# Down projection of a gated MLP: from one output pair at a time to one key at a time, with products summed in PSUM

## Chip, cores and metric

The kernel runs on one NeuronCore of a Trainium2 chip. The metric is the device time of one execution in microseconds (us). Before the change it took 1750.57 us (median of 3 runs, 1750.38 to 1752.44).

## The reference

One decoder layer over 1024 tokens (and 16 meta tokens) of width 1024: a projection, three parallel branches, a merge, an output projection, and then the MLP, which the change concerns.

```python
def rms_norm(x, g):
    xf = x.astype(jnp.float32)
    y = xf * lax.rsqrt(jnp.mean(xf * xf, axis=-1, keepdims=True) + EPS)
    return (y * g.astype(jnp.float32)).astype(x.dtype)
...
    hn = rms_norm(h, norm2_g)
    gate, up = jnp.split(hn @ w_gate_up, 2, axis=-1)
    return h + (jax.nn.silu(gate) * up) @ w_down
...
    return rms_norm(h, final_g)[:, N_META:]
```

`w_down` is 2816 x 1024. The result of `@ w_down` is added to the residual `h`, and the sum is normalised over the 1024 features of each token.

## The kernel before

Everything is kept transposed: features on partitions, tokens along the free dimension, in two halves of 512 tokens (`ch` 0 and 1). Every float32 factor is split in a high half, rounded to the matmul's format (ScalarE, a cast), and a low half, the rest (VectorE, a subtraction, L295, in `factor` and `sub_lo`); a product of two split factors takes three matmuls (L268, L269, L270 in `gemm`).

The MLP multiplies 2 x 2 blocks by seven products in place of eight. A block product is one call of `gemm`: four 128-deep steps (three in the last group) of three matmuls each. Its weight factor is one of seven sums of the four weight blocks of an output pair (features `o` and `o + 4`, in units of 128), and its other factor is one of seven **keys**: `B11`, `B21`, `T1`, `B22`, `T2`, `T3`, `T4`, sums of the four activation blocks. The products are numbered 0 to 6 like the keys in `keys`.

The loop over `f` (L2153 on) computes gate and up, 21 steps of seven products, and writes the key tiles (one per key and per pair `p` of feature blocks, 128 x 512) to DRAM: products of activations in `put`, their four sums in `act_sums` on GpSimd, the stores through `stores` on the SP queue. The down projection follows in the same loop. Its 11 pairs `p` form three **groups** (`GR`: 4, 4 and 3 pairs). For a group, all its key tiles (28, or 21) are resident; for each of four output pairs, the seven products run over the group, and `consume_down` adds them to the four result tiles of the pair in SBUF, some through VectorE from PSUM (L1825), some through GpSimd from a temporary (L2010). The weight sums of a pair are made on GpSimd in `pair_sums` (L1909 to L1912), three to four products ahead (`AHEAD`).

When the last output pair of a group starts, `next_group` queues the loads of all the next group's keys into the same buffers, key by key as each is used for the last time, and `split_x` splits a tile at each step of a product (L2090 on ScalarE, L295 on VectorE, every fourth tile on GpSimd). Tiles of `T2`, `T3` and `T4` have their low halves in buffers named `y`; `whi`, `wlo`, `op` are buffers of weight factors; `sw` are weight sums, `raw` loaded weights, `h` and `y` results, `c` temporaries.

In the last group five products per pair run over all 1024 tokens' results as usual. The other two (keys `B21` and `T4`) come at the very end for all four pairs, for tokens 0 to 255 and then 256 to 511 of the first half, with 256-column matmuls. Around them stands the final norm: squares on ScalarE, column sums on TensorE against a column of ones (L1642), the root (L593 to L598), a transposed broadcast on TensorE (L1661), scaling (L2124, L2126) and stores, for the three parts (`ALL1` and two of 256 tokens) one after another.

The program gives the order on each engine by the order in which it is written (`manual_schedule`); every engine and every DMA queue works in order.

## Time and profile before

| | us |
|---|---|
| median of 3 runs | 1750.57 |
| profiled execution, its own time | 1750.45 |
| its span, first to last instruction | 1748.7 |
| TensorE busy | 1667.2 (95%) |
| VectorE busy | 1344.6 (77%) |
| GpSimd busy | 881.0 (50%) |
| ScalarE busy | 763.0 (44%) |
| mean granted TensorE clock | 0.984 |

Durations come from the profiled execution, whose time is within 0.2 us of the median. In rows of single instructions the columns are start, duration, engine, line, operation, output <- inputs, count, and in brackets the idle time before it with what ended it. In rows of groups they are the same names, then busy time and mean in ns, then idle time. In rows of stretches: the window, its length, busy time and number of instructions of PE (TensorE), PEld (weight loads), DVE (VectorE), ACT (ScalarE) and POOL (GpSimd), the granted clock, the share of the DMA engines and GB/s. TensorE's matmuls are pipelined, so their durations overlap, and the distance of two starts is the pace.

### The profile page before, as it was taken

Reading aid. Unit: us, or ns where it says so; the run is one execution under the profiler, and the core shown is the slowest. Engines: PE = TensorE matmul, PEld = TensorE weight load, DVE = VectorE, ACT = ScalarE, POOL = GpSimd, SP = SyncE. Lnnn points to the kernel's source line nnn. Section 1 sums busy time; section 2 is a strip of 40 time slices with the busy share of each in tenths; the row PEclk is TensorE's granted clock in tenths of the full one; section 3 lists DMA queues with packets and bytes.
Section 4 is the critical chain, followed back from the end, with each engine's and each line's share of the span. In section 5 each row is a group of like instructions: output and inputs, shape, how many; then the busy total and the mean of one; then the engine's idle time right before and its main releaser. Section 6 shows DMA issues by size and latency. Waiting matters only on the chain.

```text
span 1748.7 us, 22588 instructions
## 1 busy us (share of the span) xinstructions
PE 1667.2 (95%) x7912; PEld 1383.0 (79%) x7912; DVE 1344.6 (77%) x2100; ACT 763.0 (44%) x1439; POOL 881.0 (50%) x639
## 2 busy tenths in 40 slices
PE   6989999998999999999999998999999999898986
PEld 5778878886888887888778876788888888686866
DVE  7999996588888744888886248777777777979697
ACT  4566217456544444876622234323322324443343
POOL 4322325315555665211174136766666665697664
PEclk9989999999999999999999998999999999999998
DMA  4111123233323333310285431332333226453423
GB/s 148 49 37 33 40 85 108 69 127 101 115 97 112 118 109 119 89 53 1 85 286 184 160 102 38 109 115 91 102 103 126 93 95 233 152 199 121 145 97 115
DMA packets 91922, 190.65 MB, mean 109 GB/s; under 512 B 9552, under 2 KB 21840, under 8 KB 91808
## 3 DMA queue, kind: packets, MB, share of 16 engines
q1 hardware_dynamic: 88704, 184.13, 31.7%
q10 hardware_dynamic: 2992, 4.75, 0.7%
q8 instruction: 62, 1.02, 0.2%
q0 software_dynamic: 112, 0.33, 0.1%
q14 instruction: 52, 0.43, 0.1%
HBM read 135.43 MB, written 53.74 MB: 108 GB/s over the span
## 4 chain that ended last, share of the span: by engine, by line
PE 62%; DVE 7%; DMA 2%; issue 2%; ACT 1%; POOL 1%; DVEq 0%; ACTq 0%; SPq 0%; POOLq 0%
PE ps L268 18%; PE ps L270 18%; PE ps L269 18%; PE ps L1446 2%; DMA y<-T 1%; DVE y L295 1%; PE ps L1422 1%; PE ps L1423 1%; PE ps L1421 1%; PE ps L1470 1%; PE ps L1471 1%; PE ps L1472 1%; DVE y L1712 1%; DVE h L1825 1%; DMA s<-y 1%
## 5 line engine op out<-in xcount | busy, mean ns | idle before, releaser
L268 PE MATMUL ps<-xh,whi 128*128 128x512 f32 (+1 forms) x492 | 175.0, 356 | 4.7 <-DVE u L863 2.4
L270 PE MATMUL ps<-xh,wlo 128*128 128x512 f32 (+1 forms) x492 | 173.9, 354 | 1.1 <-DVE wlo L239 1.1
L269 PE MATMUL ps<-xl,whi 128*128 128x512 f32 (+1 forms) x492 | 174.0, 354 | 0.6 <-POOL xl L295 0.4
L1825 DVE TENSOR_TENSOR c<-c,ps 128x512 f32<-128x512 f32 x175 | 119.4, 682 | 54.3 <-PE ps L270 49.6
L1847 POOL TENSOR_TENSOR h<-c,c 128x512 f32<-128x512 f32 x44 | 68.9, 1585 | 120.8 <-issue 75.1
L1834 ACT ACTIVATE c<-c 128x512 f32<-128x512 f32 x44 | 27.8, 632 | 207.5 <-DVE c L1825 207.5
L268 PEld LDWEIGHTS ps<-xh,whi 128*128 128x128 f32 x492 | 93.6, 190 | 17.8 <-DVE u L863 2.7
L270 PEld LDWEIGHTS ps<-xh,wlo 128*128 128x128 f32 x492 | 93.7, 190 | 14.9 <-DVE wlo L239 1.9
L269 PEld LDWEIGHTS ps<-xl,whi 128*128 128x128 f32 x492 | 93.7, 191 | 13.3 <-POOL xl L295 1.3
L239 POOL TENSOR_TENSOR wlo<-raw,whi 128x1024 fp32r<-128x1024 f32 x21 | 51.7, 2461 | 98.9 <-ACT whi L233 98.9
L269 PE MATMUL ps<-l,whi 128*128 128x512 f32 x232 | 90.9, 392 | 1.3 <-DVE l L295 1.2
L268 PE MATMUL ps<-h,whi 128*128 128x512 f32 x232 | 91.0, 392 | 0.0
L270 PE MATMUL ps<-h,wlo 128*128 128x512 f32 x232 | 90.6, 391 | 0.0
L720 DVE TENSOR_SCALAR_CACHE_REDUCE B<-sc,s 128x912 bf16<-128x912 f32 (+2 forms) x93 | 89.0, 957 | 0.1
L295 DVE TENSOR_TENSOR wlo<-sw,wlo 128x512 fp32r<-128x512 f32 (+1 forms) x49 | 57.1, 1165 | 22.7 <-ACT wlo L1782 19.5
L295 DVE TENSOR_TENSOR op<-raw,op 128x512 fp32r<-128x512 f32 (+1 forms) x42 | 56.3, 1352 | 17.0 <-ACT op L1047 17.0
L295 DVE TENSOR_TENSOR whi<-sw,whi 128x512 fp32r<-128x512 f32 (+1 forms) x50 | 50.6, 1013 | 24.4 <-ACT whi L1782 21.5
L295 DVE TENSOR_TENSOR op<-sw,op 128x512 fp32r<-128x512 f32 (+1 forms) x48 | 52.0, 1088 | 20.1 <-ACT op L1782 19.5
L295 DVE TENSOR_TENSOR whi<-raw,whi 128x512 fp32r<-128x512 f32 (+1 forms) x40 | 53.2, 1331 | 14.2 <-ACT whi L1047 12.7
L2010 POOL TENSOR_TENSOR h<-h,c 128x512 f32<-128x512 f32 x27 | 43.8, 1636 | 31.3 <-DVE c L1825 23.7
L1132 ACT COPY c<-ps 128x512 f32<-128x512 f32 x52 | 30.4, 585 | 63.8 <-PE ps L270 63.7
L1453 POOL CAST pm<-pm 16x512 fp32r<-16x512 f32 x14 | 8.5, 604 | 97.2 <-ACT pm L1449 97.2
(615 smaller groups left out, 5710.8 us busy)
## 6 DMA issues: line engine op xcount, KB each, us to landing
raw<-in_wts_dram SPq DMA_DIRECT2D x136, 512.0 KB, 3.9
T<-h SPq DMA_DIRECT2D x44, 256.0 KB, 5.3
B<-h SPq DMA_DIRECT2D x33, 256.0 KB, 2.0
y<-T SPq DMA_DIRECT2D x33, 256.0 KB, 5.7
y<-b SPq DMA_DIRECT2D x32, 256.0 KB, 2.2
s<-y SPq DMA_DIRECT2D x32, 256.0 KB, 4.9
ga<-c SPq DMA_DIRECT2D x16, 256.0 KB, 3.9
gb<-c SPq DMA_DIRECT2D x16, 256.0 KB, 4.1
```

What stands on the lines that cost most here:

```text
L239: e.tensor_tensor(l[:, c], r[:, c], h[:, c].bitcast(F32), op=ALU.subtract)
L268: nc.tensor.matmul(ps[:, :n], wh, xh, start=(start and k == 0), stop=False, **kw)
L269: nc.tensor.matmul(ps[:, :n], wh, xl, start=False, stop=False, **kw)
L270: nc.tensor.matmul(ps[:, :n], wl, xh, start=False, stop=(stop and k == last), **kw)
L295: getattr(self.nc, eng).tensor_tensor(lo, x, hi.bitcast(F32), op=ALU.subtract)
L720: nc.vector.tensor_scalar(junk2[:, :nk_of(i)], self.sc[i], value, None, op0=ALU.is_ge, op1=ALU.add, accum_out=at(cs, i))
L1132: nc.scalar.copy(t, ps)
L1446: nc.tensor.transpose(p3[:rows, h, :], d["S"][h][:, col:col + rows], self.ident)
L1825: nc.vector.tensor_tensor(dst, a, b, op=ALU.add)
L1834: nc.scalar.activation(t, t, AF.Silu)
L1847: nc.gpsimd.tensor_tensor(t, u, s, op=ALU.mult)
L2010: nc.gpsimd.tensor_tensor(a, a, b, op=ALU.add)
```

## The change

The down projection gets a loop of its own. Its order is now group, key, output pair: a key of a group serves all four pairs in four successive products (**slots**), and then its tiles are done with. Three sets of key buffers rotate (`B11`, `B21`, `T1`), and a table of events (`when`, `run_events`) issues loads at given slots: key tiles one per slot, two keys ahead, and their split three slots after the load at the earliest, at two places of a product. Weight blocks are loaded singly, and their sums are made in place on GpSimd (`down_sums`, `down_factor`), four per pair and group as before.

Each pair has three PSUM chains per group. Products 0, 4, 5 and 6 are added up in one bank, 2 and 3 in another, and 1 has its own. After every product `evict` adds the bank as it then stands to the one result tile that needs this partial sum (`TILE`), on VectorE; the adds of `consume_down` on GpSimd are gone. A product may write a bank only after the eviction of the product before it in that bank.

The keys run in the order `DOWN` (0, 4, 5, 6, 1, 2, 3). Of the last group, the first token half is finished after product 1 and is normalised and stored during the last keys (`out0`). The last key (product 3, which completes features 0 to 511 of the second token half) runs in two token parts of 256, each with four products; the first part's column sums stand in the second part. The outputs read the broadcast scale straight from PSUM; only one pair of outputs at the end goes through ScalarE and GpSimd.

The core of the diff:

```diff
-ORDERS = ((0, 1, 2, 3, 4, 5, 6), (0, 1, 6, 2, 3, 4, 5), (0, 2, 3, 4, 5))
-ALL1 = (1, 0, 512)
-PARTS = (ALL1, (0, 0, 256), (0, 256, 256))
+ORDERS = ((0, 1, 2, 3, 4, 5, 6), (0, 1, 6, 2, 3, 4, 5))
+DOWN = (0, 4, 5, 6, 1, 2, 3)
...
-            nc.tensor.matmul(ps[:, :n], wh, xh, start=(start and k == 0), stop=False, **kw)
...
+            nc.tensor.matmul(ps[:, c0:c0 + n], wh, xh, start=(start and k == 0), stop=False, **kw)
...
-        plans = [(j, 512) for j in range(1, NFF)] + [(NFF + 4 * g + o, P * len(GR[g])) for g in range(len(GR)) for o in range(4)]
+        plans = [(j, 512) for j in range(1, NFF)]
...
+        def weight_tile(kind, o):
+            return self.t(self.xb, [P, 512], tag={"12": "T2h", "21": "T4h", "22": "B22h", "s2": "B22l"}[kind] + str(o))
+
+        def load_w(g, kind, o):
+            n = len(GR[g]) * P
+            off = self.at["wd", (g, o + 4 * (kind[0] == "2"))]
+            src = self.a["wts"][off:off + 2 * n * P].rearrange("(p n) -> p n", p=P)
+            if kind == "11":
+                if o % 2 == 0:
+                    pair = self.t(self.wp, [P, 1024], tag="raw", bufs=2)
+                    W[g, "11", o], W[g, "11", o + 1] = pair[:, :n], pair[:, 512:512 + n]
+                t = W[g, "11", o]
...
+                t = W[g, kind, o] = weight_tile(kind, o)[:, :n]
+            c = n * (kind[1] == "2")
+            nc.sync.dma_start(t, src[:, c:c + n])
+
+        def load_x(q, k):
+            g, kk = divmod(q, NK)
+            key = ("B11", "B21", "T1")[q % 3]
+            pool = self.xb if key == "T1" else self.xap
+            hi, lo = (self.t(pool, [P, 512], F32R, tag=f"{key}{x}{k}") for x in "hl")
+            nc.sync.dma_start(lo.bitcast(F32), xd[keys[DOWN[kk]], GR[g][k]])
+            XQ.setdefault(q, []).append((hi, lo))
+            splits.append((slot, hi, lo))
+
+        def split_x(k):
+            if splits and splits[0][0] + 3 <= slot:
+                _, hi, lo = splits.popleft()
                 x = lo.bitcast(F32)
                 nc.scalar.copy(hi, x)
-                self.sub_lo(lo, x, hi, eng=eng)
+                self.sub_lo(lo, x, hi)
...
+        def down_sums(g, o):
+            pool_op(W[g, "11", o], W[g, "11", o], W[g, "21", o], ALU.subtract)
+            t = W[g, "s2", o] = weight_tile("s2", o)[:, :len(GR[g]) * P]
+            pool_op(t, W[g, "22", o], W[g, "11", o], ALU.subtract)
+
+        def down_factor(g, i, o):
+            made.append(self.factor(W[g, {0: "11", 4: "s2", 5: "11", 6: "22", 1: "12", 2: "21", 3: "s2"}[i], o]))
+            if i == 0 and o >= 2:
+                down_sums(g, o - 2)
+            elif i == 4 and o < 2:
+                down_sums(g, o + 2)
+            elif i == 5:
+                pool_op(W[g, "21", o], W[g, "21", o], W[g, "22", o], ALU.add)
+            elif i == 1:
+                pool_op(W[g, "s2", o], W[g, "12", o], W[g, "s2", o], ALU.subtract)
...
+        for g in range(NG):
+            for i in DOWN:
+                for o in range(4):
+                    thunks.append(lambda g=g, i=i, o=o: down_factor(g, i, o))
+        for o in range(4):
+            when(-14 + o, load_h2, "11", o)
+            when(-11 + o, load_h2, "12", o)
+            when(-7 + o // 2, load_w, 0, "11", o)
+            when(-4 + o // 2, load_w, 0, "21", o)
+            when(-2 + o // 2, load_w, 0, "22", o)
+            when(1 + o, load_h2, "22", o)
+            when(4 + o, load_h2, "21", o)
+            when(8 + o, load_w, 0, "12", o)
+            for g in range(1, NG):
+                t = SLOTS * (g - 1) + o
+                when(t + 11, load_w, g, "11", o)
+                when(t + 15, load_w, g, "22", o)
+                when(t + 18, load_w, g, "21", o)
+                when(t + 22, load_w, g, "12", o)
+        for q in range(NG * NK):
+            for k in range(len(GR[q // NK])):
+                when(-6 + k // 2 if q == 0 else -3 + k if q == 1 else 4 * (q - 2) + k, load_x, q, k)
...
+        TILE = {0: (0, 0), 1: (0, 0), 4: (0, 1), 3: (0, 1), 5: (4, 1), 2: (4, 1), 6: (4, 0)}
+
+        def evict(g, i, o, ps):
+            squares()
+            d, ch = TILE[i]
+            t = h2[o + d, ch]
+            nc.vector.tensor_tensor(t, ps, t, op=ALU.add)
+            if g == NG - 1 and i in (6, 1, 2):
+                sqs.append((o + d, ch))
+
...
+        def stat(accs):
+            return self.row_rstd(accs, self.const)
...
+        def bcast(st, n):
+            ps = self.ps()
+            for j in range(n // P):
+                nc.tensor.transpose(ps[:, j * P:(j + 1) * P], st[:, 8 + j:9 + j].to_broadcast([P, P]), self.ident)
+            return ps
...
+        def out0(o):
+            x = h2[o, 0]
+            nc.vector.scalar_tensor_tensor(x, x, self.cols["fg"][:, o:o + 1], rbs[0], op0=ALU.mult, op1=ALU.mult)
+            nc.sync.dma_start(self.a["out"][o * P:(o + 1) * P, :512], x)
...
+                self.later.append(lambda f=f, i=i: consume(f, i))
+
+        banks = {}
+        for slot in range(NG * SLOTS - 4):
+            g, r = divmod(slot, SLOTS)
+            kk, o = divmod(r, 4)
+            i, q = DOWN[kk], NK * g + kk
+            n_done += 1
+            ahead(n_done - 1 + AHEAD)
+            run_events()
...
+            at = {k: lambda k=k: split_x(k) for k in (0, 2)}
+            if g == NG - 1 and r == 22:
+                at[0] = lambda: sts.update({0: stat([held[0, 1], held[0, 0]])})
+            if g == NG - 1 and r == 23:
+                at[1] = lambda: rbs.update({0: bcast(sts[0], 512)})
+                at[2] = lambda: [out0(x) for x in range(2)]
+            chain = (g, o, 0 if i in (0, 4, 5, 6) else i if i == 1 else 2)
+            old = banks.get(chain)
+            ps = banks[chain] = self.gemm(made.popleft(), XQ[q], 512, at, ps=old, start=old is None, add=old is not None)
+            self.later.append(lambda g=g, i=i, o=o, ps=ps: evict(g, i, o, ps))
...
+        def finish(part, o, ps):
+            c = slice(256 * part, 256 * part + 256)
+            squares()
+            t = h2[o, 1][:, c]
+            nc.vector.tensor_tensor(t, ps[:, c], t, op=ALU.add)
+            sq = sq1[part, o] = ct()[:, :256]
+            nc.scalar.activation(sq, t, AF.Square)
+
+        def stat1(part):
+            sts[1, part] = stat([held[1, 1][:, 256 * part:256 * part + 256]] + [sq1[part, o] for o in range(4)])
+
...
+        todo = {(0, 0): {0: lambda: [out0(x) for x in (2, 3)]}, (0, 1): {0: lambda: out0(4)},
+                (0, 2): {0: lambda: out0(5), 1: prescale}, (0, 3): {0: lambda: out0(6)}, (1, 0): {1: lambda: out0(7)},
+                (1, 1): {1: lambda: stat1(0)},
+                (1, 3): {0: lambda: rbs.update({(1, 0): bcast(sts[1, 0], 256)})}}
+        for part in range(2):
+            c = slice(256 * part, 256 * part + 256)
             for o in range(4):
-                for j, kk in enumerate(("B21", "T4")):
-                    ps = self.gemm(two[o][j], xs[kk], n, at.get((key, o, j)))
-                    self.later.append(lambda o=o + 4 * j, ps=ps, key=key: finish(o, ps, key))
-                for x in after.get((key, o), ()):
-                    out(*x)
+                xs = [(h[:, c], l[:, c]) for h, l in XQ[q]]
+                ps = banks[g, o, 2]
+                self.gemm(fac[o], xs, 256, todo.get((part, o)), ps=ps, start=False, add=True, c0=256 * part)
+                self.later.append(lambda part=part, o=o, ps=ps: finish(part, o, ps))
```

On VectorE, at the first change from the old to the new group, stood these rows before (low halves of key tiles `B22l`, `y` with `T2h` and `T3h`, of factors `wlo`, `whi`, and an addition to a result `y04`):

```order
L295 TENSOR_TENSOR B22l2_2686_13345<-B22l2_2686_13345,B22h2_2685_13344 128x512
L295 TENSOR_TENSOR wlo_2715_13438<-sw_2666_13270,wlo_2715_13438 128x512
L295 TENSOR_TENSOR y14_2695_13383<-y14_2695_13383,T2h0_2694_13382 128x512
L295 TENSOR_TENSOR y15_2697_13386<-y15_2697_13386,T2h1_2696_13385 128x512
L295 TENSOR_TENSOR y16_2699_13389<-y16_2699_13389,T2h2_2698_13388 128x512
L295 TENSOR_TENSOR whi_2718_13466<-sw_2665_13269,whi_2718_13466 128x512
L295 TENSOR_TENSOR y00_2708_13427<-y00_2708_13427,T3h0_2707_13426 128x512
L295 TENSOR_TENSOR y01_2710_13430<-y01_2710_13430,T3h1_2709_13429 128x512
L1825 TENSOR_TENSOR y04_2619_13130<-y04_2619_13130,ps_2716_13441 128x512
L295 TENSOR_TENSOR y02_2712_13433<-y02_2712_13433,T3h2_2711_13432 128x512
L295 TENSOR_TENSOR wlo_2720_13492<-sw_2667_13271,wlo_2720_13492 128x512
```

At the change from the first to the second group stand now (`T1l` and `B11l` are key tiles, the L2108 rows evictions, `op`, `whi`, `wlo` factors):

```order
L288 TENSOR_TENSOR T1l0_2736_13652<-T1l0_2736_13652,T1h0_2735_13651 128x512
L2108 TENSOR_TENSOR y02_2710_13508<-ps_2694_13409,y02_2710_13508 128x512
L288 TENSOR_TENSOR op_2748_13740<-T2h3_2731_13627,op_2748_13740 128x512
L288 TENSOR_TENSOR T1l1_2740_13676<-T1l1_2740_13676,T1h1_2739_13675 128x512
L2108 TENSOR_TENSOR y03_2714_13532<-ps_2699_13433,y03_2714_13532 128x512
L288 TENSOR_TENSOR op_2753_13765<-T4h0_2647_13225,op_2753_13765 128x512
L288 TENSOR_TENSOR T1l2_2743_13699<-T1l2_2743_13699,T1h2_2742_13698 128x512
L2108 TENSOR_TENSOR y04_2591_12978<-ps_2752_13749,y04_2591_12978 128x512
L288 TENSOR_TENSOR whi_2758_13789<-T4h1_2648_13227,whi_2758_13789 128x512
```

Eight low halves of key tiles stood close together among two factors; now one key tile, one eviction and one factor take turns.

On the SP queue, in the last output pair of the old group, stood these loads of key tiles and weights before (the last row is a store of an activation product):

```order
L213 DMA raw_2690_13353<-in_wts_dram 128x1024
L2079 DMA y14_2695_13383<-T20_1961_9837 128x512
L2079 DMA y15_2697_13386<-T21_1962_9838 128x512
L2079 DMA y16_2699_13389<-T22_1963_9839 128x512
L2079 DMA y17_2701_13392<-T23_1964_9840 128x512
L2079 DMA y00_2708_13427<-T30_1972_9848 128x512
L2079 DMA y01_2710_13430<-T31_1973_9849 128x512
L2079 DMA y02_2712_13433<-T32_1974_9850 128x512
L2079 DMA y03_2714_13436<-T33_1975_9851 128x512
L1842 DMA B2210_1960_9836<-h17_2705_13411 128x512
```

In the fifth to eighth slot of the down projection stand now (`y00` to `y02` and `y13` are residual tiles, `B11l` key tiles of the fourth key, and the L1835 rows the stores of the last four activation sums):

```order
L2004 DMA y13_2702_13456<-h17_1804_9141 128x512
L2028 DMA B11l0_2704_13459<-T40_1983_9859 128x512
L1835 DMA T110_1949_9825<-h06_2692_13403 128x512
L1835 DMA T210_1971_9847<-h16_2693_13404 128x512
L1835 DMA T310_1982_9858<-h13_2629_13158 128x512
L1835 DMA T410_1993_9869<-h03_2630_13161 128x512
L2004 DMA y01_2706_13484<-h05_1799_9136 128x512
L2028 DMA B11l1_2708_13487<-T41_1984_9860 128x512
L2004 DMA y02_2710_13508<-h06_1800_9137 128x512
L2028 DMA B11l2_2712_13511<-T42_1985_9861 128x512
L2004 DMA y03_2714_13532<-h07_1801_9138 128x512
```

Key tiles came eight in a row, limited by their buffers; now they alternate with other loads, and three of the fourth key stand behind the four stores, which wait for GpSimd.

On VectorE, near the end of the program, stood these rows before (L2186 adds a product of 256 columns to a result, L2126 scales an output, L594 to L598 are the root):

```order
L2186 TENSOR_TENSOR h05_2625_13142<-ps_3103_15260,h05_2625_13142 128x256
L2186 TENSOR_TENSOR h02_2737_13585<-ps_3105_15274,h02_2737_13585 128x256
L2186 TENSOR_TENSOR h06_2739_13589<-ps_3109_15306,h06_2739_13589 128x256
L2186 TENSOR_TENSOR h03_2764_13732<-ps_3111_15320,h03_2764_13732 128x256
L2126 SCALAR_TENSOR_TENSOR y05_2620_13132<-y05_2620_13132,cols_33_115,B11l2_3112_15321 128x512
L2126 SCALAR_TENSOR_TENSOR h11_2624_13140<-h11_2624_13140,cols_33_115,B11l2_3112_15321 128x512
L2186 TENSOR_TENSOR h07_2766_13736<-ps_3115_15341,h07_2766_13736 128x256
L2186 TENSOR_TENSOR y04_2619_13130<-ps_3117_15359,y04_2619_13130 128x256
L2126 SCALAR_TENSOR_TENSOR h13_2765_13734<-h13_2765_13734,cols_33_115,B11l2_3112_15321 128x512
L2126 SCALAR_TENSOR_TENSOR y07_2622_13136<-y07_2622_13136,cols_33_115,B11l2_3112_15321 128x512
```

Now, from the first scaled output on (L2125 scales an output of the first token half from PSUM, L2108 and L2210 are evictions of 512 and 256 columns, L288 the low half of the last weight factor):

```order
L2125 SCALAR_TENSOR_TENSOR y04_2591_12978<-y04_2591_12978,cols_33_115,ps_2995_15123 128x512
L2125 SCALAR_TENSOR_TENSOR y05_2597_13004<-y05_2597_13004,cols_33_115,ps_2995_15123 128x512
L288 TENSOR_TENSOR whi_2997_15142<-B22l3_2925_14716,whi_2997_15142 128x384
L2125 SCALAR_TENSOR_TENSOR y06_2601_13026<-y06_2601_13026,cols_33_115,ps_2995_15123 128x512
L2125 SCALAR_TENSOR_TENSOR y07_2606_13049<-y07_2606_13049,cols_33_115,ps_2995_15123 128x512
L2108 TENSOR_TENSOR y13_2702_13456<-ps_2994_15119,y13_2702_13456 128x512
L2125 SCALAR_TENSOR_TENSOR y00_2701_13454<-y00_2701_13454,cols_33_115,ps_2995_15123 128x512
L2210 TENSOR_TENSOR h01_2605_13047<-ps_2983_15049,h01_2605_13047 128x256
L2125 SCALAR_TENSOR_TENSOR y01_2706_13484<-y01_2706_13484,cols_33_115,ps_2995_15123 128x512
L2210 TENSOR_TENSOR h11_2613_13075<-ps_2986_15068,h11_2613_13075 128x256
L2125 SCALAR_TENSOR_TENSOR y02_2710_13508<-y02_2710_13508,cols_33_115,ps_2995_15123 128x512
L2210 TENSOR_TENSOR h05_2616_13093<-ps_2989_15087,h05_2616_13093 128x256
```

Eight scaled outputs of 512 columns stand among the evictions whose squares the first part's column sums need.

More of the change, by code (lines that the diff above doesn't have):

```diff
@@ L2168, in mlp @@
                         stores.popleft()()
-                since += 1
-                if g == 0:
-                    self.later.append(lambda o=o, i=i: consume(o, i))
-                else:
-                    self.later.append(lambda g=g, o=o, i=i: consume_down(g - 1, o, i))
-                if j == len(steps) - 1 and n == 2:
-                    two = [self.last_factor(o) for o in range(2)]
-            if last:
-                X = XG[g]
-        a, b, c = PARTS
-        two += [self.last_factor(o) for o in range(2, 4)]
@@ L2250, in _layout @@
     for kind, arg, kt in unit_plan():
[L2251 removed]
+        if kind == "again":
             continue
```

264 lines of the change are left out of this document (87 added, 177 removed).

## Prediction

> **What bounds the kernel now.** I read three views in this order: the slices of the page (tenths of 40 slices that TensorE is busy), then stretches of ten microseconds, then the TensorE rows at the places where those stretches are thin.
>
> ```profile
> PE   6989999998999999999999998999999999898986
> ```
>
> TensorE is the bound almost everywhere; only slices 34 to 40, the down projection, dip repeatedly. The rows of stretches (TensorE, weight loads, VectorE, ScalarE, GpSimd busy, granted clock, DMA) show where:
>
> ```profile
> 1490.00:1500.00 10.00, 5.41 (x22) 3.51 (x21) 8.38 (x12) 3.70 (x8) 2.56 (x2) 1.00 1.01 345
> 1500.00:1510.00 10.00, 7.55 (x24) 5.41 (x24) 9.93 (x11) 8.33 (x17) 6.37 (x4) 0.83 0.32 120
> 1510.00:1520.00 10.00, 8.32 (x35) 6.55 (x36) 10.00 (x14) 0.63 (x1) 7.37 (x5) 1.00 0.01 2
> ...
> 1580.00:1590.00 10.00, 8.18 (x34) 5.78 (x32) 9.88 (x11) 6.47 (x12) 9.22 (x5) 1.00 0.91 324
> 1590.00:1600.00 10.00, 6.79 (x27) 5.00 (x28) 10.00 (x12) 3.99 (x8) 6.97 (x5) 1.00 0.01 2
> 1600.00:1610.00 10.00, 10.00 (x45) 8.29 (x45) 10.00 (x13) 3.69 (x7) 9.84 (x7) 1.00 0.32 105
> ...
> 1660.00:1670.00 10.00, 6.36 (x25) 3.99 (x23) 10.00 (x9) 8.23 (x17) 8.76 (x6) 1.00 0.63 233
> 1670.00:1680.00 10.00, 9.82 (x35) 7.56 (x36) 9.97 (x18) 0.70 (x3) 2.26 (x2) 0.83 0.25 82
> ```
>
> A full stretch holds 45 or 46 matmuls, the thin ones 22, 24, 35, 34, 27, 25 and 35. The three dips are the three changes of group, with VectorE busy for 8.38 to 10.00 of 10 us in each. The chain of waits names what is there:
>
> ```profile
> 1478.43 6.04 DMA y<-T
> ...
> 1488.35 4.07 DVE y L295 x3
> ```
>
> All 28 tiles of the next group (seven keys by four) are reloaded and split within the last output pair of the old one, so DMA comes first, then VectorE (L295, the low halves). How much this costs follows from the pace of TensorE:
>
> ```profile
> 1485.98 0.39 PE L268 MATMUL ps<-B11h,wlo 128*128 128x512 f32 x1
> ...
> 1488.70 0.39 PE L268 MATMUL ps<-B21h,op 128*128 128x512 f32 x1
> ...
> 1735.05 0.28 PE L268 MATMUL ps<-B21h,T1h 128*128 128x256 f32 x1
> ...
> 1737.09 0.28 PE L270 MATMUL ps<-T4h,B22l 128*128 128x256 f32 x1
> ```
>
> Twelve matmuls of 512 columns take 1488.70 - 1485.98 = 2.72 us, 0.2267 each; the last seventeen steps of 256 take 1737.09 - 1735.05 = 2.04, 0.12 each. The down projection begins at 1485.98, its last matmul is through at 1737.21, and 11.5 us follow to the span's 1748.7. Its work is 852 x 0.2267 + 144 x 0.12 = 210.4 us, so 1737.21 - 1485.98 - 210.4 = **40.8 us are lost**: 57 missing matmuls at the first change (12.9 us), 30 or so at each of the others (7.0 and 7.3), some 13.6 in the tail and in thin spots.
>
> **The change, part by part.** *TensorE.* The products are the same; 888 are now 512 wide and 72 are 256 wide: 201.3 + 8.6 = **209.9 us**, 0.5 less. A product of two 512 x 512 blocks ("slot") lasts 2.72 us in groups 1 and 2, 2.04 in group 3.
>
> *Key tiles.* A key now serves four outputs, then its buffers are free, and tiles come two keys ahead, one per slot, split three slots (8.2 us) later:
>
> ```profile
> y<-T SPq DMA_DIRECT2D x33, 256.0 KB, 5.7
> ```
>
> 5.7 us from issue to landing, the slowest of these loads now, fit in 8.2 (6.1 in group 3), and one tile per slot is what VectorE has to split. So the cause of the three dips goes, and the second and third I price at 1 us together (0 to 14.3). What is late next is VectorE.
>
> *VectorE and GpSimd.* Per slot VectorE makes one eviction, the low half of one factor and that of one key tile:
>
> ```profile
> 1486.00:1738.00 252.00, 229.08 (x1038) 186.61 (x1036) 213.76 (x270) 101.34 (x196) 176.67 (x120) 0.97 0.39 136
> 1486.00:1738.00 252.00, 139.98 (x141) 0.97 0.39 136
> L1825 DVE TENSOR_TENSOR h<-h,ps 128x512 f32<-128x512 f32 x39 | 25.7, 678 | 8.4 <-PE ps L270 7.6 <-DMA B11l<-B 0.9
> L295 DVE TENSOR_TENSOR wlo<-sw,wlo 128x512 fp32r<-128x512 f32 (+1 forms) x17 | 20.7, 1217 | 3.8 <-ACT wlo L1782 3.8
> L295 DVE TENSOR_TENSOR T1l<-T1l,T1h 128x512 fp32r<-128x512 f32 x9 | 5.9, 679 | 1.2 <-DMA y<-T 1.2
> L1912 POOL TENSOR_TENSOR sw<-raw,raw 128x512 f32<-128x512 f32 (+1 forms) x12 | 18.4, 1529 | 0.0
> ```
>
> An eviction takes 0.68. A low half takes 0.68 at best and 140.0 / 141 = 0.99 on average (the second row is L295 alone) while GpSimd is busy for 176.7 of 252 us, 70%. GpSimd loses the adds of the old consumption; 48 weight sums (a quarter shorter in group 3), nine adds of squares and the last four sums of activations stay, about 91 us of 224, 41%. A low half then takes about 0.68 + 0.31 x 41 / 70 = 0.86, and a slot 0.68 + 2 x 0.86 = 2.40 of 2.72 us; in group 3 (three-quarter factors, three tiles in four slots) 0.68 + 0.65 + 0.65 = 1.98 of 2.04. VectorE fits, without room at the end.
>
> What separates 0.68 from 1.2 is GpSimd's presence: VectorE's 1.77 us row starts inside GpSimd's 1.73.
>
> ```profile
> 1522.69 1.73 POOL L1857 TENSOR_TENSOR h<-h,h 128x512 f32<-128x512 f32 x1
> 1523.20 1.77 DVE L295 TENSOR_TENSOR wlo<-sw,wlo 128x512 fp32r<-128x512 f32 x1
> ```
>
> The Trainium skill, page "SBUF — State Buffer", section "Who interferes with whom", says that a VectorE instruction with two SBUF inputs and a GpSimd one that reads SBUF shut each other out for a whole instruction, and that one with a single SBUF input is spared. By that rule evictions keep 0.68 beside any GpSimd work, as their row has it; if they stretched like low halves, to 0.86, a slot of group 3 would be 2.16 of 2.04 and the sum 28 x 0.12 = 3 us longer.
>
> *Moved at no cost.* Weights come as single halves, and with the residual tiles the SP queue has 18 more transfers in all; the 0.39 of DMA share in the row above hides them, and if SP is late instead, that is rival 2. ScalarE's squares and the early output of the first token half lie beside TensorE's last keys (ScalarE is busy for 101 of 252 us); what they cost VectorE is in the tail below.
>
> *Start of the stage (first change).* Two things crowd there: eight weight sums, two products and four activation sums on GpSimd, 14 x 1.53 = 21 us, and SP, which stands at the stores of those last sums before it may issue the next key tiles. VectorE and ScalarE then wait for these in order, with evictions behind them; four banks in rotation allow three slots, 8.2 us. From 0 (hidden) to the old 12.9 us; I take 4, nearer the hidden end, since GpSimd's 21 us start about one slot ahead and the stores are clear at some 20 us, the tiles at 26, and the fourth key is first used after 12 slots, 32.6 us.
>
> *Tail.* Now:
>
> ```profile
> 1715.80 1.87 PE L1642 MATMUL ps<-ones,B11l 128*128 128x1 f32 x8 [3.94 <-POOL B11l L2010]
> ...
> 1719.24 0.56 PE L268 MATMUL ps<-B21h,T1h 128*128 128x256 f32 x1
> ...
> 1725.36 0.31 PE L268 MATMUL ps<-B21h,T1h 128*128 128x256 f32 x1
> ...
> 1728.97 0.50 PE L1642 MATMUL ps<-ones,B11h 128*128 128x1 f32 x4
> ...
> 1730.47 0.36 PE L268 MATMUL ps<-B21h,T1h 128*128 128x256 f32 x1
> ```
>
> After the wait of 3.94 us, 24 matmuls of 256 columns and four transposes took 1725.36 - 1719.24 = 6.1 us, the matmuls alone being worth 24 x 0.12 = 2.9: waits of this size also cost clock. The first dip has the same pair, a wait and then the granted clock of 0.83 in its stretch:
>
> ```profile
> 1498.53 0.50 PE L268 MATMUL ps<-T1h,whi 128*128 128x512 f32 x1 [2.89 <-ACT whi L1782]
> ```
>
> The Trainium skill, page "TensorE: Matmul & The Clock Gate", section "What's actually happening", gives half the clock after an idle window of about 3.4 us; by that rule a new wait of 3 us would cost no clock and the sum would be 3 us lower, by the row with 2.89 us it may cost some.
>
> In the new tail: 18 column sums at 1.50 / 12 = 0.125 and six transposes, 3.3 us. The sums of the last key's first part stand in its second part. From the broadcast of the first half's scale to there TensorE has some 6.4 us of matmuls, VectorE eight scaled outputs and two evictions at 0.68, two low halves at 0.65 and four half evictions at about 0.42, 9.8 us: 3.4 late. It also brings a debt from the nine slots before, where GpSimd's 13 adds cost it 13 x (1.22 - 0.68) = 7.0 us against a reserve of 9 x 0.34 = 3.1 (a slot there is 1.70 with idle GpSimd): 3.9. Of 7.3 I take 6, since the earlier sums give some back; the bounds are 0, all hidden, and 14, where each add costs 1.77 - 0.68. Then TensorE runs 3 us longer on a low clock, as it does now (0 to 5). The end after the last matmul has the same links (sums, root, transposes, scaling, store), with scaling straight from PSUM: 11.0 instead of 11.5.
>
> **Sum:** 209.9 + 4 + 1 + 3.3 + 6 + 3 + 11.0 = 238.2 us from 1485.98, a span of 1724.2. The profiled execution took 1750.45 for a span of 1748.7, so 1726.0 us; the median of before, 1750.57, is the same within 0.1. What precedes 1485.98 keeps its instructions, so I leave it.
>
> **The rivals.**
> 1. *No stall left.* All waits hide: 209.9 + 3.3 + 1 + 10.5 = 224.7, 1712.4 us. For it: 2.40 of 2.72; against it: 1.98 of 2.04.
> 2. *The start keeps its stall.* The stores of the activation sums hold SP, and the first change still costs 12.9: 1735 us. For it: SP's order; against it: keys two ahead.
> 3. *The bank waits for VectorE (slower).* An output's bank takes its next product only after its eviction. If low halves cost the 1.22 us of `wlo<-sw`, a slot is 0.68 + 2 x 1.22 = 3.12 of 2.72, and in group 3 about 2.5 of 2.04; beyond three slots of debt TensorE goes at that pace: 56 x 0.40 + 24 x 0.46 = 33 us, some 1759 us. It decides from a low half of 1.02 us (a slot of 2.72), against 0.99 now at 70% GpSimd. The Trainium skill, "PSUM — Partial Sum Buffer", section "Summary: rules for kernel authors", says to read another bank than the one matmuls write, which is this wait told as a rule.
>
> **How the numbers follow.** Forecast (1718 to 1731) 0.55; rival 1 (to 1718) 0.17; rival 2 and a partly late VectorE (1731 to 1747) 0.18; between 1747 and 1754 0.04; rival 3 0.06. A difference under 0.2%, 3.5 us, is about what a measurement of this kernel cannot tell from none. Faster 0.90, same 0.04, slower 0.06. The range takes rival 1's time and most of rival 2's: 1712 to 1743.
>
> **What would show it.** In the new profile the stretches after 1490 should hold 45 matmuls without dips at 1580 and 1660; the eviction row should stay near 680 ns and the low halves fall to about 0.86 us; GpSimd should fall to about 41%; one wait of the column sums should stand in the last 25 us. I am wrong if TensorE waits for evictions in the middle of a group, if L295 stays near 1 us, or if SP's stores open a hole around 1510.

## The result and the profile after

The changed kernel takes 1719.64 us (median of 4 runs, 1717.17 to 1720.82) against 1751.17 us for the kernel before (1750.38 to 1752.44): a ratio of 0.9817 with a 95% interval of 0.98 to 0.9834. Forecast were 1726.0 us, between 1712 and 1743: the gain is 31.5 us where 24.6 to 25.2 were expected. The profiled execution took 1719.94 us for a span of 1718.2. Lines have moved by seven: the low halves' L295 is now L288, the column sums' L1642 is L1635, evictions are L2108.

First the slices, then the stretches of ten microseconds (TensorE, weight loads, VectorE, ScalarE, GpSimd, granted clock, DMA):

```profile
PE   6989999998999999999999997999999999999998
```

```profile
1490.00:1500.00 10.00, 10.00 (x45) 8.26 (x44) 9.86 (x11) 2.13 (x4) 8.06 (x6) 1.00 0.51 170
1500.00:1510.00 10.00, 8.23 (x36) 6.49 (x35) 10.00 (x9) 4.79 (x9) 9.92 (x6) 1.00 0.47 174
1510.00:1520.00 10.00, 9.52 (x40) 7.09 (x39) 10.00 (x12) 5.19 (x9) 8.24 (x6) 1.00 1.00 351
...
1580.00:1590.00 10.00, 10.00 (x46) 8.29 (x45) 10.00 (x13) 4.58 (x8) 4.73 (x3) 1.00 0.29 96
1590.00:1600.00 10.00, 10.00 (x46) 8.29 (x45) 8.61 (x16) 4.05 (x8) 0.00 (x0) 1.00 0.32 94
...
1660.00:1670.00 10.00, 10.00 (x46) 8.29 (x45) 8.00 (x14) 3.62 (x7) 0.00 (x0) 1.00 0.37 118
```

Slices 35, 37 and 39, which dipped before, are as full as the others. The changes of group at 1580 and 1660 hold 46 matmuls per stretch, as many as any other place. Of the first change a thin place is left, 36 and 40 instead of 45, with VectorE busy for all 20 us and GpSimd for 18.

GpSimd's and VectorE's share, the low halves alone, and the evictions (two stretch views, and a group of the page):

```profile
1487.00:1709.00 222.00, 219.71 (x1024) 183.46 (x1022) 192.08 (x269) 97.70 (x181) 90.76 (x61) 0.99 0.45 148
1487.00:1709.00 222.00, 133.21 (x154) 0.99 0.45 148
L2108 DVE TENSOR_TENSOR y<-ps,y 128x512 f32<-128x512 f32 x60 | 41.1, 686 | 19.6 <-PE ps L263 19.6
```

GpSimd is busy for 90.76 of 222 us, 41%. A low half takes 133.21 / 154 = 0.865 us and an eviction 0.686. The forecast had 41%, 0.86 and 0.68.

The thin place at the start, TensorE's rows first, then VectorE, GpSimd and SyncE:

```profile
1487.08 0.39 PE L261 MATMUL ps<-B11h,wlo 128*128 128x512 f32 x1
...
1502.16 0.50 PE L262 MATMUL ps<-B21l,wlo 128*128 128x512 f32 x1 [1.77 <-DVE B21l L288]
...
1511.38 0.47 PE L261 MATMUL ps<-T1h,op 128*128 128x512 f32 x1 [0.31 <-DVE h L2108]
...
1514.08 0.50 PE L262 MATMUL ps<-T1l,op 128*128 128x512 f32 x1 [0.17 <-DVE T1l L288]
```

```profile
1496.95 1.78 DVE L288 TENSOR_TENSOR B21l<-B21l,B21h 128x512 fp32r<-128x512 f32 x1
...
1500.36 1.75 DVE L288 TENSOR_TENSOR B21l<-B21l,B21h 128x512 fp32r<-128x512 f32 x1
```

```profile
1496.55 1.62 POOL L2040 TENSOR_TENSOR B22l<-B22h,raw 128x512 f32<-128x512 f32 x1
...
1499.97 1.59 POOL L2040 TENSOR_TENSOR B22l<-B22h,raw 128x512 f32<-128x512 f32 x1
1501.52 1.74 POOL L1850 TENSOR_TENSOR h<-h,h 128x512 f32<-128x512 f32 x1
```

```profile
1503.29 5.44 SPq L1835 DMA_DIRECT2D T<-h  x4
```

TensorE reaches the second key's fourth tile (B21) at 1500.2. VectorE begins its low half only at 1500.36, inside a GpSimd add (1499.97 to 1501.56), and needs 1.75 us for it; TensorE loses 1.9 us. Two shorter waits, for an eviction (the bank) and for a tile, follow at 1511 and 1514. SyncE does stand at the stores of the last activation sums until they begin at 1503.29, as the second rival said; the holes name VectorE.

The tail, TensorE's rows and then two stretches of 2 us:

```profile
1687.59 2.04 PE L1635 MATMUL ps<-ones,h 128*128 128x1 f32 x16
...
1694.15 0.28 PE L261 MATMUL ps<-T1h,op 128*128 128x256 f32 x1
...
1699.89 0.50 PE L1635 MATMUL ps<-ones,h 128*128 128x1 f32 x4
1700.25 2.01 PE L1635 MATMUL ps<-ones,c 128*128 128x1 f32 x16
...
1702.74 0.41 PE L262 MATMUL ps<-T1l,whi 128*128 128x256 f32 x1
...
1704.88 0.41 PE L263 MATMUL ps<-T1h,wlo 128*128 128x256 f32 x1
...
1706.81 0.50 PE L1635 MATMUL ps<-ones,h 128*128 128x1 f32 x4
```

```profile
1702.00:1704.00 2.00, 2.00 (x13) 2.00 (x13) 1.30 (x7) 0.42 (x2) 0.00 (x0) 0.65 0.20 69
1704.00:1706.00 2.00, 2.00 (x12) 2.00 (x11) 0.75 (x3) 0.74 (x3) 0.00 (x0) 0.50 0.00 0
```

No row up to the last product carries a wait. The 36 instructions of column sums take 4.1 us, and from 1702.6 to 1705.9 a matmul takes 0.213 instead of 0.12 us at a granted clock of 0.50. The last product is through at 1706.81, and the end takes 11.39 us.

What VectorE and ScalarE did behind the broadcast of the first half's scale, up to the squares that the first part's column sums need (L2212):

```profile
1692.95 1.41 DVE L2125 SCALAR_TENSOR_TENSOR y<-y,cols,ps 128x512 f32<-128x512 f32 x2 [0.42 <-PE ps L2118]
...
1700.68 0.42 DVE L2210 TENSOR_TENSOR h<-ps,h 128x256 f32<-128x256 f32 x1
```

```profile
1701.19 0.42 ACT L2212 ACTIVATE c<-h 128x256 f32<-128x256 f32 x1 [0.57 <-DVE h L2210]
```

The terms of the forecast beside what this execution shows:

| term | forecast us | measured us |
|---|---|---|
| stage begins | 1485.98 | 1487.08 |
| matmuls, 888 x 0.2267 + 72 x 0.12 | 209.9 | 209.9 |
| start of the stage | 4 | 3.3 |
| other changes of group | 1 | 0 |
| column sums and transposes ahead of the last product's end | 3.3 | 4.8 |
| wait for VectorE in the tail | 6 | 0 |
| low clock and slow starts after the sums | 3 | 1.7 |
| end | 11.0 | 11.4 |
| from the stage's begin to the span's end | 238.2 | 231.1 |

### The profile page after: what moved, and what is told of

It is laid out like the page before. It is cut to its first block, busy times and chain, and to the rows that moved or that the text cites. A ratio compares the mean times of both kernels' runs of the same rounds, so it can differ in the third digit from the quotient of the medians.

```text
span 1718.2 us, 22508 instructions
## 1 busy us (share of the span) xinstructions
PE 1656.6 (96%) x7888; PEld 1377.3 (80%) x7888; DVE 1322.5 (77%) x2104; ACT 753.6 (44%) x1415; POOL 789.4 (46%) x577
## 3 DMA queue, kind: packets, MB, share of 16 engines
q8 instruction: 62, 1.02, 0.2%
## 4 chain that ended last, share of the span: by engine, by line
PE 66%; DVE 5%; issue 2%; ACT 1%; POOL 1%; DMA 0%; SPq 0%; DVEq 0%; ACTq 0%; POOLq 0%
PE ps L261 19%; PE ps L263 19%; PE ps L262 19%; PE ps L1439 2%; PE ps L1415 1%; PE ps L1416 1%; PE ps L1463 1%; PE ps L1414 1%; PE ps L1464 1%; PE ps L1465 1%; DVE y L1705 1%; DVE T1l L288 1%; DVE l L288 1%; PE ps L1635 0%; PE ps L1472 0%
## 5 line engine op out<-in xcount | busy, mean ns | idle before, releaser
L1818 DVE TENSOR_TENSOR c<-c,ps 128x512 f32<-128x512 f32 x151 | 103.3, 685 | 49.0 <-PE ps L263 44.3
L288 DVE TENSOR_TENSOR whi<-raw,whi 128x512 fp32r<-128x512 f32 (+1 forms) x40 | 52.5, 1313 | 15.6 <-ACT whi L1040 13.0
L288 DVE TENSOR_TENSOR op<-raw,op 128x512 fp32r<-128x512 f32 (+1 forms) x38 | 49.0, 1301 | 16.4 <-ACT op L1040 16.4
L2040 POOL TENSOR_TENSOR raw<-raw,T4h 128x512 f32<-128x512 f32 (+1 forms) x12 | 18.8, 1568 | 89.9 <-DVE op L288 48.5
L1451 ACT CAST ph<-ps 128x512 fp32r<-128x512 f32 x72 | 42.1, 588 | 33.4 <-PE ps L1439 33.0
L2108 DVE TENSOR_TENSOR y<-ps,y 128x512 f32<-128x512 f32 x60 | 41.1, 686 | 19.6 <-PE ps L263 19.6
L262 PEld LDWEIGHTS ps<-l,whi 128*128 128x128 f32 x232 | 43.6, 188 | 12.4 <-DVE l L288 2.8
L1120 DVE TENSOR_TENSOR c<-ps,c 128x512 f32<-128x512 f32 x45 | 30.9, 687 | 29.3 <-PE ps L263 25.9
```

Of the source, the lines that this page charges most:

```text
L262: nc.tensor.matmul(ps[:, c0:c0 + n], wh, xl, start=False, stop=False, **kw)
L288: getattr(self.nc, eng).tensor_tensor(lo, x, hi.bitcast(F32), op=ALU.subtract)
L1120: nc.vector.tensor_tensor(dst, ps, t, op=ALU.add)
L1451: nc.scalar.copy(ph[:rows], ps[:rows])
L1818: nc.vector.tensor_tensor(dst, a, b, op=ALU.add)
L2108: nc.vector.tensor_tensor(t, ps, t, op=ALU.add)
```

## The experiments

Single runs of one kernel differ by up to 3.65 us here (the four of the changed kernel), partly ahead of the stage: it began between 1485.54 and 1489.95 in the runs below, which change next to nothing before it. So runs that differ by little are compared from the first product of the stage on, in the profile. "Lost at the start" adds up what the distances of neighbouring matmuls in the first 40 us exceed 0.2267 us by, over the distances of 0.24 us and more.

| run | time us | stage begins | lost at the start | last key | end | stage in all |
|---|---|---|---|---|---|---|
| changed kernel | 1719.94 | 1487.08 | 3.25 | 12.66 | 11.39 | 231.1 |
| a_stores | 1719.79 | 1486.41 | 3.75 | 12.65 | 11.34 | 231.6 |
| a_sumslate | 1718.55 | 1487.96 | 2.82 | 11.11 | 11.11 | 228.8 |
| a_start | 1723.81 | 1489.95 | 4.24 | 12.64 | 11.33 | 232.1 |
| a_late | 1716.30 | 1486.18 | 1.96 | 11.12 | 11.30 | 228.2 |
| a_late_early | 1716.41 | 1485.85 | 2.54 | 11.11 | 11.29 | 228.8 |
| a_fold | 1718.05 | 1487.56 | 2.70 | 10.94 | 11.11 | 228.5 |
| a_best (profiled) | 1716.60 | 1485.54 | 2.09 | 12.47 | 10.76 | 229.2 |
| a_whole | 1721.24 | 1487.34 | 2.20 | | | 232.1 |
| a_ballast2 | 1730.26 | 1486.78 | 3.73 | 11.07 | 11.35 | 241.7 |
| a_jit | 1732.45 | 1488.09 | 7.34 | 11.20 | 11.36 | 242.6 |

The start is the same up to 1508 in the changed kernel, a_fold, a_whole and a_ballast2, and a_fold and a_whole leave the first 40 us alone altogether. Still the loss there is 3.25 us in the changed kernel, 2.70 in a_fold and 2.20 in a_whole: the hole at 1502 (in the changed kernel's time) is 1.77 us wide in the changed kernel and 0.71 in the other three. A difference of about 1 us at the start is therefore within what equal instructions give.

**What the time before was lost to.** Two edits of the kernel before, one for each theory. The first takes out GpSimd's adds in `consume_down`:

```diff
-                pool_add(c11, b["p1"])
...
-                pool_add(c12, b["u"])
...
-                    pool_add(c22, u)
-                    pool_add(c21, u)
```

> The kernel before, without the 40 GpSimd adds of the down projection's results (four per output pair in groups 1 and 2, two in group 3; the outputs lack these terms). Loads, splits and order stay. GpSimd's busy share from 1486 to 1738 falls from 70% to about 46%. Theory R (the time was lost because 28 key tiles are reloaded and split in one output pair): the three thin stretches stay, only VectorE's share of them shrinks, 40 x 0.37 us = 15 us of VectorE at most, of which about half lies in them: 1737 to 1744 us. Theory G (GpSimd's adds slowed VectorE, and their going is the gain): the thin stretches nearly close and the time comes to 1720 to 1728 us.

1746.38 us against 1750.32 on the same chip: 3.9 us less than before, which is less than either theory gave. The stage began 2.2 us later here (1488.21 against 1485.98); from its first product to the span's end it is 256.4 us against 262.7, 6.3 less, at the lower edge of theory R's range. The stretches around the first two changes of group, of the kernel before:

```profile
1500.00:1520.00 20.00, 15.87 (x59) 11.96 (x60) 19.93 (x24) 8.95 (x18) 13.74 (x9) 0.91 0.16 61
...
1580.00:1600.00 20.00, 14.96 (x61) 10.78 (x60) 19.88 (x22) 10.46 (x19) 16.19 (x9) 1.00 0.46 163
```

and without the adds:

```profile
1500.00:1520.00 20.00, 12.90 (x37) 9.34 (x38) 19.59 (x18) 11.45 (x22) 14.20 (x9) 0.78 0.30 109
...
1580.00:1600.00 20.00, 18.15 (x77) 13.81 (x75) 19.15 (x25) 10.47 (x19) 10.05 (x6) 1.00 0.60 211
```

The second change gains 16 of the 29 matmuls that were missing from 90; the first loses 22 more in this window, with a lower clock. So most of the loss does not go with GpSimd's adds. The other edit leaves out the reload:

```diff
-            X1 = XG[g] = {key: [] for key in keys}
+            XG[g] = X
+            return
```

> The kernel before, with the key tiles of the first group kept for all three groups: no reload and no split at a change of group (42 low halves of VectorE and 7 of GpSimd or more fall away, the outputs are computed from the wrong activations), GpSimd's adds stay. Theory R: the three thin stretches go, 12.9 + 7.0 + 7.3 = 27.2 us, the tail's 13.6 us stay: 1720 to 1727 us. Theory G: GpSimd's adds go on slowing VectorE, so that half of the loss or more stays: 1735 us or more.

1717.76 against 1750.32 us, 32.6 less; the same two stretches:

```profile
1500.00:1520.00 20.00, 20.00 (x90) 16.57 (x89) 13.08 (x17) 5.37 (x9) 19.42 (x13) 1.00 0.46 159
...
1580.00:1600.00 20.00, 20.00 (x90) 16.57 (x89) 9.61 (x15) 4.74 (x8) 13.02 (x9) 1.00 0.21 70
```

Both are full, although GpSimd is busier in the first than before. Theory R holds, and by 2 us more than its range: some of the 13.6 us that the forecast put down to the tail also came from the reload, since the wait of the column sums there, 3.94 us before, is

```profile
1685.73 1.05 PE L1642 MATMUL ps<-ones,B11l 128*128 128x1 f32 x8 [1.76 <-POOL B11l L2010]
```

The edit takes out loads and splits together and does not part them. It spares VectorE the splits, which the change only spreads; so it says what the bunch cost, not what spreading must bring.

**What GpSimd's relief is worth in the new order.** The changed kernel with a load put back on GpSimd:

```diff
+            if 8 <= slot and slot % 2 == 0:
...
+                pool_op(ballast[0], ballast[0], ballast[1], ALU.add)
```

> The changed kernel with one more GpSimd add of 512 columns, on tiles that nobody else reads, in every second slot from the ninth on (36 adds of about 1.55 us, 56 us): GpSimd's share of 1486 to 1709 rises from 41% to about 66%, near the 70% of before. Theory R: VectorE pays 36 x 0.37 to 0.70 us = 13 to 25 us, against some 30 us that it idles there, and TensorE loses 0 to 8 us: 1719 to 1728 us. Theory G, and the third rival of the prediction: low halves pass 1.02 us, the banks wait for evictions, and most of the gain is given back: 1735 us or more.

1730.26 us, 10.3 more, between the theories. Low halves alone, then two of the waits:

```profile
1487.00:1709.00 222.00, 160.61 (x154) 0.98 0.42 140
```

```profile
1529.30 0.47 PE L261 MATMUL ps<-B11h,op 128*128 128x512 f32 x1 [0.47 <-DVE y L2108]
...
1698.30 1.87 PE L1635 MATMUL ps<-ones,h 128*128 128x1 f32 x8 [4.00 <-POOL h L2040]
```

and, ahead of the second, the add that it waits for and the eviction that this goes back to:

```profile
1696.86 1.39 POOL L2040 TENSOR_TENSOR h<-h,c 128x512 f32<-128x512 f32 x1 [1.96 <-ACT c L2092]
```

```profile
1695.38 0.68 DVE L2108 TENSOR_TENSOR y<-ps,y 128x512 f32<-128x512 f32 x1
```

A low half now takes 160.61 / 154 = 1.043 us. VectorE pays (160.61 - 133.21) / 36 = 0.76 us for each add, more than the 0.70 at which the expectation ended. Past the 1.02 us that the third rival named, banks wait for evictions, half a microsecond or so at a time: some 5.3 us are lost in the middle of the stage, about 3.2 of them at five such waits, the rest at low halves and short waits. The largest part of what remains is a 4.00 us wait of the column sums. It names GpSimd, but GpSimd itself sat idle for 1.96 us until the square came, and the square's tile was evicted only at 1695.38, by a VectorE that had been busy without a break since 1675.8: VectorE's debt again. So the third rival's mechanism is there and its point is borne out by this one run, and its price of 33 us was for a slower low half (1.22 us). The relief gave little by itself (3.9 us in the old order, 6.3 from the first product on), but without it the new order gives back 10.3.

**What the lead of two keys is worth.**

```diff
-... else 4 * (q - 2) + k, load_x, q, k)
+... else 4 * (q - 1) if q < 20 else 4 * (q - 2) + k, load_x, q, k)
```

> The changed kernel with the tiles of keys 3 to 20 loaded all at once in the first slot of the key before, and split three slots later as now: two tiles in the last slot of the old key, the others during the first product of the new one, as late as can be. Work, GpSimd and the order of products stay. If the lead over the first use is what closed the thin stretches (theory R), each of 18 keys waits for ScalarE and VectorE, 1.5 us or more: 1745 us or more. If the order by keys with a bank per output closes them by itself, the slots behind hide it: 1725 us or less.

1732.45 us, 11.5 more from the first product on; neither branch. Some of the waits:

```profile
1516.11 0.50 PE L262 MATMUL ps<-T1l,op 128*128 128x512 f32 x1 [2.40 <-DVE T1l L288]
...
1587.25 0.50 PE L262 MATMUL ps<-T1l,op 128*128 128x512 f32 x1 [1.37 <-DVE T1l L288]
...
1588.94 0.50 PE L262 MATMUL ps<-T1l,op 128*128 128x512 f32 x1 [0.73 <-DVE T1l L288]
```

and a stretch right behind the last two:

```profile
1589.50:1592.50 3.00, 3.00 (x8) 2.32 (x8) 2.27 (x3) 1.66 (x3) 0.52 (x1) 0.50 0.00 0
```

Waits stand at about six of the 18 keys, where VectorE is crowded. At the others, tiles that are split during the product that reads them still come in time. Some 3 us of the loss are clock: twice, behind two waits close together, matmuls go at half pace for about 3.3 us. So the order by keys closes part of the thin stretches alone; the lead and the loading of one tile per slot, both of which the edit takes away, are worth a third of the gain together.

**The start: SyncE or VectorE.** First the stores later:

```diff
-            if slot in (1, 4, 7):
+            if slot in (1, 10):
```

> The changed kernel with the stores of the last four activation sums issued at the eleventh slot instead of the fifth, so that SyncE does not stand at them from 1498.5 to 1508.8 us ahead of the next loads. Second rival of the prediction (SyncE's order makes the stall of the start): the holes at 1502, 1511 and 1514 us, 3.3 us together, go. Theory V (VectorE, slowed by GpSimd, is behind with the splits): they stay within 0.5 us, with VectorE busy for 10 of 10 us there.

```profile
1500.68 0.50 PE L262 MATMUL ps<-B21l,wlo 128*128 128x512 f32 x1 [0.96 <-DVE B21l L288]
```

1719.79 us, 3.75 lost at the start: the hole at 1500 is shorter by 0.8 us, and waits for evictions further on make up for it. Moving SyncE's stand won nothing, so its order is not what binds. Then the sums themselves:

```diff
-            if slot == 2:
+            if slot == 18:
...
-            if slot in (1, 4, 7):
+            if slot in (1, 4, 20):
```

> The changed kernel with the last four activation sums on GpSimd moved from the third to the nineteenth slot, where GpSimd idles, and their stores behind them. Theory V (VectorE, slowed by GpSimd, makes the start's stall of 3.3 us): VectorE gains about 4 x 0.76 us between 1501 and 1509, so the holes at 1511 and 1514 go, and that at 1502, whose cause lies ahead of these sums, stays: 1.5 to 2.5 us remain. If the sums have nothing to do with it, 3.3 us remain.

2.82 us stayed lost, a miss: the sums still ran in the crowded place. GpSimd does not wait for slots; it had only swapped them with the weight sums behind, so that they began at 1519.7 instead of 1501.5, 18 us later and not 16 slots (43 us). The next edit adds an earlier second key (`-5 + k` for `-3 + k`):

> The same, and the second key's tiles are loaded and split two slots earlier, where VectorE idles 3.2 us (1481.3 to 1484.5). Theory V: the hole at 1502 goes too, 0 to 0.7 us of 3.3 remain, and the time comes to 1715.5 to 1717.5 us. If something else holds the fourth tile of that key, 1.5 us or more remain.

A miss too. The hole at 1502 is gone, but five waits for evictions came in its place, the longest

```profile
1523.39 0.47 PE L261 MATMUL ps<-T1h,whi 128*128 128x512 f32 x1 [0.94 <-DVE h L2108]
```

and 4.24 us were lost. VectorE's work was moved, not made less. So the sums were put out of the start altogether:

```diff
-            if slot == 2:
+            if slot == 42:
...
-            if slot in (1, 4, 7):
+            if slot in (1, 4, 47):
```

> The changed kernel with the last four activation sums on GpSimd behind the weight sums of the second group (43rd slot), where GpSimd idles for 50 us, and their stores at the 48th slot. In the run before this one they had only changed places with the weight sums behind them, and still ran from 1520 to 1526 us. The stage, from its first product to the span's end, is 231.1 us with the change, 3.25 of them lost in its first 40 us. Theory V: VectorE has 4 x 0.76 = 3 us less to do there; the hole at 1502, whose cause lies ahead, stays, the others go: about 2.0 lost. If GpSimd's share there does not matter: 3.25.

```profile
1500.62 0.50 PE L262 MATMUL ps<-B21l,wlo 128*128 128x512 f32 x1 [1.12 <-DVE B21l L288]
```

1.96 us lost, the total of theory V, and 1716.30 us. The sums ran from 1579 to 1586, out of the start. But the parts are not theory V's. The hole at 1502, which it leaves alone, is 1.12 us instead of 1.77, and without any edit at the start it was as short as

```profile
1501.37 0.50 PE L262 MATMUL ps<-B21l,wlo 128*128 128x512 f32 x1 [0.71 <-DVE B21l L288]
```

in a_whole. Of the other two holes, that at 1511, which should have gone, stayed (0.31 us). Only that at 1514 went, as it did in a_sumslate and a_best, while it stands in the five runs with the sums and the second key in their place; with the slower matmuls behind it, it cost about 0.6 us. So the four sums are worth about 0.6 us, and that the total agreed was luck. With the earlier second key as well:

> The same, with the second key's tiles loaded and split two slots earlier. With that alone the hole at 1502 was gone, and VectorE's debt came out in five waits for evictions between 1509 and 1527, 4.2 us lost. Theory V: the debt shrinks by the 3 us of the four sums: 0.5 to 1.5 lost. If VectorE is late there for another reason than GpSimd: 3 or more.

2.54 us, between the two branches and above theory V's 1.5: 1.7 less than the 4.24 of a_start, by single runs, and about 2.5 remain. What they come from (the ten other adds on GpSimd, or VectorE's own work, which still holds the last products of the up projection) stays open; the weight sums there could not be moved, since the next key's factors need them.

**The tail.** The column sums thinned out:

```diff
+            acc = sq1[0, 0] if part == 0 else held[1, 1][:, c]
+            if (part, o) in ((0, 1), (0, 2), (1, 0), (1, 1), (1, 2)):
+                pool_op(acc, acc, sq, ALU.add)
...
-            sts[1, part] = stat([held[1, 1][:, 256 * part:256 * part + 256]] + [sq1[part, o] for o in range(4)])
+            h = held[1, 1][:, 256 * part:256 * part + 256]
+            sts[1, part] = stat([h, sq1[1, 3]] if part else [h, sq1[0, 3], sq1[0, 0]])
...
-                (0, 2): {0: lambda: out0(5), 1: prescale}, (0, 3): {0: lambda: out0(6)}, (1, 0): {1: lambda: out0(7)},
-                (1, 1): {1: lambda: stat1(0)},
+                (0, 2): {1: prescale}, (1, 0): {2: lambda: out0(5)},
+                (1, 1): {2: lambda: [out0(6), out0(7), stat1(0)]},
```

> The changed kernel with the squares of the last key added on GpSimd ahead of the column sums (12 and 8 TensorE instructions instead of 20 and 20), and three scaled outputs of the first token half moved behind the evictions of the first part. 20 instructions less are 20 x 0.112 = 2.2 us. Theory C (a row of 20 column sums brings the granted clock to half from 1702.6 to 1706): with 12 the clock stays and 1.8 us more go, 3.5 to 4 in all, 1715.5 to 1716.5 us. Theory D (the clock falls there for another reason): 1.5 to 2.2 us, 1717.5 to 1718.5 us, and a stretch of the last part at 0.21 us a matmul is still there.

1718.05 us. The last key took 10.94 us without a drop of the clock, but a_sumslate, a_late and a_late_early, whose last key is that of the change, took 11.11 to 11.12 without one as well. So the fold gave 0.2 us there and 0 to 0.2 at the end (11.11 us against 11.11 to 11.30), where the sums wait for the last square and GpSimd's add whatever their number, and theory C is not borne out. The last key in one piece:

```diff
-        for part in range(2):
...
+        for o in range(4):
+            self.gemm(fac[o], XQ[q], 512, todo.get((0, o)), ps=ps, start=False, add=True)
```

> The changed kernel with its last key in one piece of 512 tokens: column sums, scale and outputs of the second token half all come behind the last product. TensorE saves 0.5 us of narrow matmuls; the 20 instructions of column sums of the first part move behind it, where all but the last run while the last square is made; one eviction and one square are 0.26 and 0.2 longer, and six scaled outputs of 0.74 instead of 0.42 us add 1.9. If the two parts are worth what they hide: 2 to 4 us longer, 233 to 235 us from the first product on. If the narrow matmuls and the double chain of sums cost as much: 231 us or less.

```profile
1702.39 4.56 PE L1635 MATMUL ps<-ones,c 128*128 128x1 f32 x32
```

1721.24 us. Its stage of 232.1 us has 2.2 lost at the start and no drop of the clock ahead of the end. Without the loss at the start that is 229.9, and 226.3 for the two parts (a_late's 228.2 - 1.96): the parts are worth about 3.6 us, within the 2 to 4, though the total lay below the 233 expected. The row shows why: 32 instructions of sums in one piece, 4.56 us, between the last product and the root.

**Both edits that shortened something**, the late sums of a_late and the fold of a_fold:

> The changed kernel with the two edits that shortened a part of its own each: the last four activation sums behind the second group's weight sums (start: 1.96 us lost instead of 3.25), and the squares of the last key added on GpSimd (last key 10.9 and end 11.1 us, against 11.1 and 11.3 in a run without the drop of the clock). If both add up: 227.8 us from the first product on, 1715 to 1716.5 us; with the drop of the clock in the last key, 1.5 us more, 1716.5 to 1718. If the adds on GpSimd and the later sums get in each other's way: as the changed kernel, 1719.6 us.

1716.08 us (median of 5, 1713.65 to 1717.37) against 1751.75 before: 0.9793, interval 0.9779 to 0.9806. That is 3.6 us below the changed kernel's median, though the two intervals touch. Its profiled run lost 2.09 us at the start and had the drop of the clock in its last key. What of this is the fold's cannot be told.

## Why the prediction was right

**What bounds the kernel.** Right. The three thin stretches were the bunch of reloads and splits (b_noreload: 32.6 us), the two later ones are gone with no rest, and TensorE sets the pace between. The forecast lay 7.1 us above the stage's 231.1; the wait in the tail (6 us) and its clock (1.3) make up that error, and the errors of the other terms, -0.7, -1, +1.5 and +0.4, cancel, which is luck.

**VectorE beside GpSimd.** Right in size: 41%, 0.865 and 0.686 us. That the low half goes with GpSimd's share held once more with the load put back: 148 of 222 us give 0.68 + 0.31 x 67 / 70 = 0.98 by the forecast's line, 1.04 were measured. The evictions kept their time beside any load, as the Trainium skill, page "SBUF — State Buffer", section "Who interferes with whom", has it for an instruction with one SBUF input; the low half of 1.78 us that begins at 1496.95, inside a GpSimd add that ends at 1498.17, and is through 0.56 us behind it, agrees with the same place.

**Start of the stage.** 3.3 of the 4 us taken, and 2.2 to 2.7 in the two runs with the same start. Of the two crowds it was the first: VectorE was late, with low halves of 1.75 to 1.78 us beside GpSimd's adds. What each of the 14 adds cost is not shown; the four that were moved away cost about 0.6 us. SyncE's stand was real, and moving it won nothing (a_stores). The second rival falls.

**Column sums.** Mis-sized: 18 sums at 0.125 us, where a sum is two instructions and the row of twelve that gave the price was six sums. The 36 instructions took 4.1 instead of 2.25 us; the transposes took 0.6.

**Tail wait: the step that failed.** Six us were forecast and none came. The debt of 3.9 us counted 13 adds on GpSimd in nine slots. Between 1672.9 and 1692 there were seven, and six stretched low halves cost about 4.5 us, against the reserve of 3.1 and 1.9 us of column sums in between: nothing was left, and VectorE stood waiting for the broadcast (0.42 us ahead of 1692.95). Of the other 3.4 us, 1.65 fell away, mostly because one of the two evictions and one of the two low halves counted there were already done, so that VectorE took 8.15 us instead of 9.8. TensorE's matmuls gave it 7.0 us instead of 6.4. The remaining 1.2 us, and 0.5 us of the last square, are hidden in the column sums: these begin at 1699.89 with what is ready, and the last square was through at 1701.61, just when they reached it. With GpSimd loaded (a_ballast2) the wait in the tail stands there, 4.00 us, at the first half's sums: the mechanism exists, its size was wrong.

**Low clock.** Forecast as a follower of that wait, 3 us; it came without one and cost 1.5 us in the last key, and 0.2 of slow starts earlier. That it came at all is chance: in five other runs with the same last key it did not.

**First and third rival.** The time lies between the forecast's middle and the first rival's 1712.4: what that one left out is the start's 3.3 us, the sums and the clock. The third rival's bound is 0.16 us of low half away, as a_ballast2 shows.

## What to carry to other kernels

When a stage keeps its engines busy on average but loses time in bunches, spread the bunch before making the bunched work cheaper: here taking work off a helper engine gave 3.9 us in the old order, taking out the bunch gave 32.6, and the change, which spreads the bunch and takes the work off as well, gave 31.5. Then look for what the spread order needs: a lead of two keys with one load per slot was worth a third of the gain, and a free GpSimd another third that shows only when it is taken away. A later place in the program need not delay an instruction as much on an engine that waits for data alone: four sums written 43 us later ran 18 us later. Look where the instruction ran.
